# Down-projection of a fourier / RG-LRU / ConvFFN block: low parts and sums on VectorE alone, first steps prepared during the last up-products

## The chip, the core and the metric

[...] The metric is device time in microseconds of one execution.

## The reference

One layer of a diffusion block over 1024 latent positions of width 1024, in float32. The change lies in its second half, the ConvFFN:

```python
def conv_ffn(h, rows, w_up, conv_w, conv_b, w_down):
    b, n, _ = h.shape
    u = (h @ w_up).reshape(b, rows, n // rows, 2 * D_FF)          # D_FF = 2816
    u = dwconv2d(u, conv_w, conv_b).reshape(b, n, 2 * D_FF)       # 3x3 depthwise on a 16 x 64 grid
    gate, val = jnp.split(u, 2, axis=-1)
    return (jax.nn.gelu(gate) * val) @ w_down
...
x = x + g2 * conv_ffn(modulate(x, norm2_g[l], sh2, sc2), rows,
                      ffn_w_up[l], ffn_conv_w[l], ffn_conv_b[l], ffn_w_down[l])
return rms_norm(x, final_g)
```

## The kernel before

**Products in three matmuls.** A float32 operand is split into a high part (a copy to the matmul type fp32r, ScalarE, `copy`, line 131) and a low part (operand minus high part, `sub`, line 138, on VectorE or GpSimd). A product is high x high + high x low + low x high.

**Seven products instead of eight.** Up- and down-projection each use a Strassen-Winograd scheme: two-by-two blocks of both operands, sums of blocks, seven block products, sums of results.

**Up-projection** (`ffn`). The 2816 gate and 2816 value channels go in 22 tiles n of 128 channels. Tile n has two PSUM tiles, `ug` (gate) and `uv` (value), of 1024 positions, and seven products i = 0 to 6 of twelve matmuls (`up_product`, line 1526). Product 6 of tile n runs after product 0 of tile n+1. `up_join` (line 1542, VectorE) adds a stored product to half a PSUM tile; `up_conv` starts the 3x3 convolution: one ScalarE instruction for the centre and eight "taps" on VectorE that read PSUM and add to the accumulator in SBUF (line 1564). `gelu` (ScalarE), then `glu` (line 1574, GpSimd) multiplies gate and value, and the result goes to DRAM, G[n] (line 1576). At the last tile `up_free` gives back the operands of a finished product and starts the loads of the down weights.

**Down-projection** (`down`). The 22 channel tiles of G form 11 pairs i of an even and an odd tile. Seven passes p, in the order `DOWN = (1, 2, 6, 7, 5, 4, 3)`, run over the 11 pairs: 77 steps s, each a 128 x 512 by 128 x 512 product with four position blocks j, twelve matmuls (`mm`, line 1792). X and Y are sets of four PSUM banks (`dn`): passes 1, 2 and then 5, 3 collect in X, passes 6, 7, 4 in Y, which begins as a copy of X after pass 1. A step's operands go through four stages, each run ahead of the matmuls by `down_until`:

- `down_load`: the weight tile (line 1679), the activations (1688, 1693, 1696), the stored sum S2 (1697), on SP's queue, up to six steps ahead;
- `down_sums`: the sums of blocks, mostly VectorE (two operations in pass 2, three in pass 6, one in passes 7, 5 and 3); one of pass 6 on GpSimd (line 1714);
- `down_hi`: two high parts on ScalarE;
- `down_lo`: two low parts, the first on GpSimd, the second on VectorE, three steps ahead.

All these buffers are 48 slots that are handed out again in the order in which they were given back. Between the stages of a step stand at most two "tasks" from a list: evacuations of PSUM, multiplications by the row g2, additions to the residual rows y (fetched from DRAM by `fetch`, line 1770), squares (ScalarE, line 1779), and `norm` (lines 1782 to 1785), the final RMSNorm of 128 positions and its store. The last four steps of pass 3 are run block by block: all matmuls of j = 0, then of j = 1 and so on, and a last block of code finishes each j.

What sets the order: each engine's list is the order in which this code calls it. In pass 1 the last taps, step by step, stand between the stages, and the last up-product stands ahead of step 0.

Of the kernel before, what the change touches and what calls it, by code (L numbers as in the profile page):

```python
# [11 lines left out]
OP = mybir.AluOpType  # L12
# [100 lines left out]
class K:  # L113
# [1471 lines left out]
    def ffn(self):  # L1585
        sl = self.sl
        self.G = [self.dp.tile([128, 1024], F32, name=f"G{n}") for n in range(NP)]
        last = NP - 1

        todo = deque([(0, 4), (0, 5), (0, 6), (1, 1), (1, 3), (1, 4), (1, 5), (1, 6)])  # L1590
        self.down_plan()
        for n in range(NP):
            if n > 1:
                self.up_banks(n)
            if n + 2 < NP and n:
                self.up_load(n + 2)
# [102 lines left out]
    def down_sums(self, s, p, i):  # L1699
# [52 lines left out]
    def down(self):  # L1752
# [4 lines left out]
        y = {}  # L1757
# [43 lines left out]
        for p in self.DOWN:  # L1801
            if p in (1, 5):
                X = banks()
            if p == 6:
                X, bank = X, Y
            bank = Y if p in (6, 7, 4) else X
            for i in range(11):
                if p == 1:
                    if i == 0:
                        self.up_product(last, 6)  # L1810
                        self.up_free(6)
                        self.up_conv(last, "v")
                    if i == 2:
                        self.glu(last - 1)
                        self.taps(last, "gt", 1)
                    self.taps(last, "gt" if i < 5 else "vt", 2 if i < 9 else 8)
                    if i == 5:
# [4 lines left out]
                self.down_until(self.down_load, s + 6 if p != 1 or i > 2 else s + 4)  # L1822
# [6 lines left out]
                if p == 7 and i == 0 or p == 5 and i == 0:  # L1829
                    pass  # L1830
                if i:
                    for _ in range(2):
                        if tasks:
                            tasks.popleft()()
                if p == 3 and i == 7:
                    for f in (self.down_hi, self.down_lo):
                        self.down_until(f, len(self.steps))
                    for j in range(4):
                        for q in range(4):
                            mm(s + q, X, [j], False, q == 3)  # L1840
# [8 lines left out]
            if p == 1:  # L1849
                Y = banks()  # L1850
                for j in range(4):
                    self.copy("act", Y[j], X[j])
            elif p == 2:
                for j in range(4):
                    c11[j] = temp(j)
                    tasks.append(lambda j=j, b=X[j]: v.tensor_tensor(c11[j], b, self.g2row[:, H[0]], op=OP.mult))
            elif p == 6:
                u = pair()
                for j in range(4):
                    self.copy("act", at(u, j), Y[j])  # L1860
            elif p == 7:
                def begin():
                    nonlocal w
# [1 line left out]
                tasks += [lambda: None] * 4 + [begin]  # L1865
                for j in range(4):
                    tasks.append(lambda j=j, b=Y[j]: self.copy("act", at(w, j), b))
            elif p == 5:
                fg = sl.get([128, 1024], any_=True)
                src = a["final_g"]  # L1870
                nc.sync.dma_start(fg, bass.AP(tensor=src.tensor, offset=src.offset, ap=[[0, 128], [1, 1024]]))
                p5 = pair()
                for j in range(4):
                    tasks.append(lambda j=j, b=X[j]: self.copy("act", at(p5, j), b))
                for j in range(4):
                    def c22(j=j):
                        g.tensor_tensor(at(w, j), at(w, j), at(p5, j), op=OP.add)
                        g.tensor_tensor(at(w, j), at(w, j), self.g2row[:, H[1]], op=OP.mult)

                    def c12(j=j):  # L1880
# [3 lines left out]
                    tasks += [c22, c12]  # L1884
                for j in range(4):
                    def adds(j=j):
                        v.tensor_tensor(y[j][:, H[1]], y[j][:, H[1]], at(u, j), op=OP.add)
                        v.tensor_tensor(y[4 + j][:, H[1]], y[4 + j][:, H[1]], at(w, j), op=OP.add)
                        square(4 + j, 1, j)
                    tasks.append(adds)  # L1890
            elif p == 4:
                r = [temp(j) for j in range(4)]
                for j in range(4):
                    tasks.append(lambda j=j, b=Y[j]: v.tensor_tensor(r[j], b, self.g2row[:, H[0]], op=OP.mult))
                for j in range(4):
                    def add(j=j):
                        v.tensor_tensor(y[4 + j][:, H[0]], y[4 + j][:, H[0]], r[j], op=OP.add)
                        square(4 + j, 0, j)
                    tasks.append(add)
                for j in range(4):  # L1900
                    tasks.append(lambda j=j: norm(4 + j))
        for j in range(4):
            r = temp(j)
            v.tensor_tensor(r, X[j], self.g2row[:, H[1]], op=OP.mult)
            v.tensor_tensor(y[j][:, H[1]], y[j][:, H[1]], r, op=OP.add)
            square(j, 1, j)
            norm(j)

    def run(self):
        self.plan()  # L1910
# [84 lines left out]
```

## Time and profile before

| | us |
|---|---|
| median of three runs (1555.39 to 1558.95) | 1557.04 |
| profiled execution, its own time | 1557.34 |
| its span, first to last instruction | 1555.5 |
| busy: TensorE / VectorE / GpSimd / ScalarE | 1408.2 / 1215.6 / 755.1 / 669.3 |
| mean granted clock of TensorE, as a share of full speed | 0.966 |

The down-projection begins at about 1272 us of the span and ends with it. "Busy" of TensorE counts modelled ends of pipelined matmuls; how fast it is fed is better read from the time that a pass takes. The mean of a whole run hides stages with different limits, so the views that follow are cut to the down-projection, and within it to passes and to single waits.

### The profile page before, as it was taken

To read this page: it belongs to the slowest core of one execution; us is meant where nothing else is said; L and a number is where in the kernel's file an instruction comes from. 1 tells how busy PE (TensorE), PEld (TensorE's weight loads), DVE (VectorE), ACT (ScalarE), POOL (GpSimd) and SP (SyncE) were. 2 spreads that over 40 slices of the span, in tenths; PEclk is the share of its full clock that TensorE was granted. 3 is DMA by queue.
4 is the path that set the end of the run, shared out by engine and by line. 5 is a ranking of instruction groups with operands and counts; after the bars stand their busy time and mean duration, and the time that the engine had idled before them with its cause. 6 is when DMAs were issued, how large, how long until landed. Compare 5 with 4: busy or idle time off the path is not lost.

```text
span 1555.5 us, 17031 instructions
## 1 busy us (share of the span) xinstructions
PE 1408.2 (91%) x6333; PEld 1126.9 (72%) x6333; DVE 1215.6 (78%) x1265; ACT 669.3 (43%) x968; POOL 755.1 (49%) x504
## 2 busy tenths in 40 slices
PE   5999999998999689979967999999999988989983
PEld 4788888877887678868845777777777767768862
DVE  5768677855116986495687999999999989799795
ACT  6566777663110213342255444444444434445441
POOL 2211311122002452392088777788777726886760
PEclk9999999999999899989988999999999998999996
DMA  9211111101115444413321112222211166422622
GB/s 374 94 34 34 35 34 41 41 28 55 41 54 180 136 126 160 154 41 122 111 80 54 66 61 78 82 82 82 82 63 64 51 243 230 183 75 102 230 88 103
DMA packets 52787, 155.21 MB, mean 100 GB/s; under 512 B 5781, under 2 KB 10192, under 8 KB 52704
## 3 DMA queue, kind: packets, MB, share of 16 engines
q1 hardware_dynamic: 51264, 151.76, 27.4%
q10 hardware_dynamic: 1184, 2.11, 0.4%
q8 instruction: 50, 0.82, 0.2%
q0 software_dynamic: 256, 0.25, 0.1%
q14 instruction: 33, 0.27, 0.1%
HBM read 131.29 MB, written 22.81 MB: 99 GB/s over the span
## 4 chain that ended last, share of the span: by engine, by line
DVE 36%; PE 13%; issue 6%; ACT 2%; POOL 1%; DMA 1%; SPq 0%; DVEq 0%; ACTq 0%; POOLq 0%
DVE s L1564 23%; PE big L194 6%; PE dn L1792 6%; DVE s L138 2%; POOL s L138 1%; DVE ug L1542 1%; DVE s L1713 1%; DVE uv L1542 1%; DVE s L1710 1%; DVE s L1225 1%; PE uv L1526 1%; DVE s L1784 1%; DMA s<-G 1%; ACT s L131 1%; DVE s L1726 1%
## 5 line engine op out<-in xcount | busy, mean ns | idle before, releaser
L138 POOL TENSOR_TENSOR s<-s,s 128x512 fp32r<-128x512 f32 (+1 forms) x288 | 462.0, 1621 | 332.4 <-ACT s L131 259.9
L194 PE MATMUL big<-s,s 128*128 128x512 f32 (+2 forms) x2352 | 559.2, 396 | 10.3 <-DVE s L138 6.5
L194 PEld LDWEIGHTS big<-s,s 128*128 128x128 f32 (+2 forms) x2352 | 438.0, 189 | 115.7 <-DVE s L138 7.8
L131 ACT ACTIVATE s<-s 128x512 fp32r<-128x512 f32 (+2 forms) x406 | 263.0, 697 | 259.8 <-DVE mid L912 61.9
L1526 PE MATMUL ug<-s,s 128*128 128x512 f32 x1056 | 263.9, 398 | 24.3 <-ACT uv L131 13.4
L138 DVE TENSOR_TENSOR s<-s,s 128x512 fp32r<-128x512 f32 (+2 forms) x150 | 189.8, 1274 | 92.1 <-ACT s L131 64.7
L1526 PEld LDWEIGHTS ug<-s,s 128*128 128x128 f32 x1056 | 197.7, 189 | 79.1 <-ACT uv L131 22.0
L1792 PE MATMUL dn<-s,s 128*128 128x512 f32 x924 | 227.9, 408 | 29.9 <-DVE s L138 15.5
L1792 PEld LDWEIGHTS dn<-s,s 128*128 128x128 f32 x924 | 180.0, 196 | 77.7 <-DVE s L138 17.5
L1564 DVE SCALAR_TENSOR_TENSOR s<-ug,rest,s 128x945 f32<-128x945 f32 (+2 forms) x176 | 214.9, 1221 | 5.3
L1564 DVE SCALAR_TENSOR_TENSOR s<-uv,rest,s 128x945 f32<-128x945 f32 (+2 forms) x176 | 214.8, 1220 | 4.6
L1526 PE MATMUL uv<-s,s 128*128 128x512 f32 x792 | 199.9, 402 | 15.3 <-DVE uv L1542 14.0
L1526 PEld LDWEIGHTS uv<-s,s 128*128 128x128 f32 x792 | 149.5, 191 | 59.1 <-DVE uv L1542 23.4
L782 POOL TENSOR_TENSOR s<-s,s 128x1280 f32<-128x1280 f32 x8 | 25.2, 3152 | 190.9 <-ACT s L778 190.9
L899 POOL TENSOR_TENSOR s<-s,s 128x1024 f32<-128x1024 f32 x8 | 21.1, 2641 | 127.4 <-PE big L194 120.7
L1474 POOL TENSOR_TENSOR s<-s,s 128x512 f32<-128x512 f32 x22 | 28.6, 1301 | 63.6 <-DMA s<-in_ffn_w_up_b_dram 63.6
L131 ACT ACTIVATE p<-uv 128x512 f32<-128x512 f32 x22 | 13.2, 599 | 105.5 <-PE uv L1526 105.5
L885 DVE TENSOR_TENSOR s<-big,s 128x1024 f32<-128x1024 f32 x8 | 9.8, 1224 | 61.1 <-PE big L194 61.1
L745 DVE SCALAR_TENSOR_TENSOR s<-big,par,s 128x1023 f32<-128x1023 f32 (+1 forms) x24 | 30.8, 1282 | 34.2 <-ACT s L742 33.6
L1574 POOL TENSOR_TENSOR s<-s,s 128x1024 f32<-128x1024 f32 x22 | 53.4, 2427 | 5.5 <-DVE s L1564 5.5
L1552 ACT ACTIVATE s<-uv,rest 128x1024 f32<-128x1024 f32 x22 | 26.6, 1208 | 48.2 <-POOL s L138 33.6
L777 ACT ACTIVATE s<-big,rest 128x1024 f32<-128x1024 f32 x32 | 35.7, 1117 | 24.6 <-PE big L194 17.8
(231 smaller groups left out, 1537.8 us busy)
## 6 DMA issues: line engine op xcount, KB each, us to landing
s<-in_mod_w_dram SPq DMA_DIRECT2D x48, 512.0 KB, 4.7
s<-in_ffn_w_up_b_dram SPq DMA_DIRECT2D x44, 512.0 KB, 4.3
s<-in_w_in_b_dram SPq DMA_DIRECT2D x32, 512.0 KB, 4.3
s<-G SPq DMA_DIRECT2D x55, 256.0 KB, 3.2
G<-s SPq DMA_DIRECT2D x22, 512.0 KB, 2.6
s<-in_ffn_w_down_dram SPq DMA_DIRECT2D x22, 512.0 KB, 5.8
s<-in_x_dram SPq DMA_DIRECT2D x16, 512.0 KB, 5.4
s<-G SPq DMA_DIRECT2D x11, 512.0 KB, 5.7
```

Source lines behind the costliest of these rows:

```text
L131: self.nc.scalar.activation(out, in_, AF.Copy)
L138: (self.nc.vector if eng == "dve" else self.nc.gpsimd).tensor_tensor(out, a, b, op=OP.subtract)
L194: return [lambda x=x: nc.tensor.matmul(x[0], x[1], x[2], start=x[3], stop=x[4]) for x in calls]
L745: nc.vector.scalar_tensor_tensor(u[:, lo:hi], z[:, lo + s:hi + s], tap[t], u[:, lo:hi], op0=OP.mult, op1=OP.add)
L777: nc.scalar.activation(lat, ps, AF.Sigmoid, bias=col)
L1474: p.tensor_tensor(u["x"][:, L], rg[:, L], rv[:, L], op=OP.subtract)
L1526: nc.tensor.matmul(o, x, y, start=first, stop=k == 3 and m == 2, skip_group_check=not fresh)
L1542: self.nc.vector.tensor_tensor(o, o, p, op=OP.add)
L1552: nc.scalar.activation(acc, ps, AF.Identity, bias=self.par["fcb"][:, ti:ti + 1], scale=self.fcw(4, ti))
L1564: nc.vector.scalar_tensor_tensor(o, i, w, o, op0=OP.mult, op1=OP.add))
L1574: nc.gpsimd.tensor_tensor(u["ga"], u["ga"], u["va"], op=OP.mult)
L1792: nc.tensor.matmul(bank[j], x, z, start=first and m == 0, stop=end and m == 2, skip_group_check=not check)
```

## The change

- **Low parts** (`down_lo`): both on GpSimd in pass 1 for the first nine pairs, both on VectorE in all other steps. The sum of pass 6 that GpSimd made (line 1714) goes to VectorE.
- **Start**: `up_free` now loads weights and activations of the first nine steps in turn, and prepares high and low parts of the first two or three. The last up-product moves from ahead of step 0 to behind it; the join of the value half moves behind that product. The taps of the last tile stand alone on VectorE up to pair 8.
- **Tasks**: the first evacuation by multiplication (`c11`) moves from after pass 2 to after pass 6; the multiplication of `u` goes from GpSimd to VectorE, behind pass 7; in pass 4 the four ScalarE copies of X are left out and VectorE adds X from PSUM; the residual rows are fetched earlier, 0 to 3 in pass 5 and 4 to 7 at the beginning of pass 4.
- **Last block**: `norm` of block j stands behind multiplication, addition and square of block j + 1.

```diff
@@ ffn
-            self.up_join(n, "v")
+            if n < last:
+                self.up_join(n, "v")
@@ up_free
-        for _ in range(3):
-            if len(self.wd) < 11:
-                self.down_weight(len(self.wd), 0)
+        n = (2, 6, 4, 8, 8, 9, 9)[i]
+        self.down_until(self.down_load, n)
+        if i in (4, 5):
+            for f in (self.down_hi, self.down_lo):
+                self.down_until(f, i - 2)
@@ down_sums, pass 6
-            self.nc.gpsimd.tensor_tensor(o[:, L], o[:, L], t[0], op=OP.subtract)
+            v.tensor_tensor(o[:, L], o[:, L], t[0], op=OP.subtract)
@@ down_lo
-        for t, f, eng in zip(self.ready[s], self.factors(s, p, i), ("pool", "dve")):
+        for t, f, eng in zip(self.ready[s], self.factors(s, p, i), ["pool" if p == 1 and i < 9 else "dve"] * 2):
@@ down
-                    if i == 0:
+                    if i == 1:
                         self.up_product(last, 6)
                         self.up_free(6)
+                        self.up_join(last, "v")
                         self.up_conv(last, "v")
                     if i == 2:
                         self.glu(last - 1)
-                        self.taps(last, "gt", 1)
-                    self.taps(last, "gt" if i < 5 else "vt", 2 if i < 9 else 8)
+                    if i < 9:
+                        self.taps(last, "gt" if i < 4 else "vt", 2 if i < 8 else 8)
...
-                    if i == 10:
+                    if i == 9:
                         self.glu(last)
...
-                if p == 4 and i in (0, 2, 4, 6):
-                    fetch(4 + i // 2)
-                    fetch(i // 2)
+                if p == 5 and i in (5, 6, 7, 8):
+                    fetch(i - 5)
+                if p == 4 and i in (0, 1, 2, 3):
+                    fetch(4 + i)
...
             elif p == 7:
...
+                for j in range(4):
+                    tasks.append(lambda j=j: v.tensor_tensor(at(u, j), at(u, j), self.g2row[:, H[1]], op=OP.mult))
             elif p == 5:
...
-                p5 = pair()
                 for j in range(4):
-                    tasks.append(lambda j=j, b=X[j]: self.copy("act", at(p5, j), b))
+                    def c22(j=j, b=X[j]):
+                        v.tensor_tensor(at(w, j), b, at(w, j), op=OP.add)
+                        v.tensor_tensor(at(w, j), at(w, j), self.g2row[:, H[1]], op=OP.mult)
+                    tasks.append(c22)
                 for j in range(4):
-                    def c22(j=j):
-                        g.tensor_tensor(at(w, j), at(w, j), at(p5, j), op=OP.add)
-                        g.tensor_tensor(at(w, j), at(w, j), self.g2row[:, H[1]], op=OP.mult)
-
-                    def c12(j=j):
-                        g.tensor_tensor(at(u, j), at(u, j), self.g2row[:, H[1]], op=OP.mult)
+                    def c1(j=j):
                         v.tensor_tensor(y[j][:, H[0]], y[j][:, H[0]], c11[j], op=OP.add)
+                        v.tensor_tensor(y[j][:, H[1]], y[j][:, H[1]], at(u, j), op=OP.add)
                         square(j, 0, j)
...
-        for j in range(4):
-            r = temp(j)
...
-            norm(j)
+        for j in range(5):
+            if j < 4:
+                r = temp(j)
...
+            if j:
+                norm(j - 1)
```

Three places show the new order. TensorE, where the up-projection ends (`uv` is the value half of the last tile, `dn` a down bank, `s_` a buffer; s_8714 is the operand of the last up-product), lines with + are new there:

```order
 L1526 MATMUL uv<-s_5758,s_8811 128x512
 L1526 MATMUL uv<-s_5757,s_8811 128x512
+L1795 MATMUL dn<-s_8943,s_8942 128x512 x12
 L1526 MATMUL uv<-s_5691,s_8714 128x512
 L1526 MATMUL uv<-s_5692,s_8714 128x512
```

Step 0 now stands between the last two up-products.

VectorE at the same place, before (L1542 the join, L1564 taps, L138 low parts of steps 0 to 2):

```order
L1542 TENSOR_TENSOR uv<-uv,u_8951 128x512
L1564 SCALAR_TENSOR_TENSOR s_8934<-ug,rest,s_8934 128x15x63
L1564 SCALAR_TENSOR_TENSOR s_8934<-ug,rest,s_8934 128x960
L138 TENSOR_TENSOR s_8983<-s_8830,s_8983 128x512
L138 TENSOR_TENSOR s_8987<-s_8832,s_8987 128x512
L138 TENSOR_TENSOR s_8991<-s_8834,s_8991 128x512
```

and now, the end of the same taps (L1708 and L1709 are the sums of pass 2, L138 the low parts of steps 9 and 10):

```order
L1564 SCALAR_TENSOR_TENSOR s_9020<-uv,rest,s_9020 128x15x63
L1564 SCALAR_TENSOR_TENSOR s_9020<-uv,rest,s_9020 128x960
L1564 SCALAR_TENSOR_TENSOR s_9020<-uv,rest,s_9020 128x15x63
L1708 TENSOR_TENSOR s_8832<-s_8832 128x512
L1709 TENSOR_TENSOR s_8830<-s_8830 128x512
L138 TENSOR_TENSOR s_9139<-s_9088,s_9139 128x512
L138 TENSOR_TENSOR s_9140<-s_9086,s_9140 128x512
L1708 TENSOR_TENSOR s_8836<-s_8836 128x512
```

No low part stands among the taps any more; the first on VectorE is that of step 9, behind all of them.

VectorE where the sums of pass 6 are made, before (L1710 and L1713 sums, L138 the second low part of a step; GpSimd makes the first and the third sum):

```order
L1710 TENSOR_TENSOR s_9424<-s_9424,s_8976 128x512
L1713 TENSOR_TENSOR s_9448<-s_9157,s_8832 128x512
L138 TENSOR_TENSOR s_9431<-s_9379,s_9431 128x512
L1710 TENSOR_TENSOR s_9448<-s_9448,s_8978 128x512
L1713 TENSOR_TENSOR s_9472<-s_9182,s_8834 128x512
```

and now (L1713, L1716, L1717 sums, L138 both low parts):

```order
L1713 TENSOR_TENSOR s_9424<-s_9424,s_8836 128x512
L1716 TENSOR_TENSOR s_9448<-s_9159,s_8834 128x512
L1717 TENSOR_TENSOR s_9159<-s_9159,s_9448 128x512
L138 TENSOR_TENSOR s_9430<-s_9381,s_9430 128x512
L138 TENSOR_TENSOR s_9431<-s_9379,s_9431 128x512
```

Three operations a step became five; GpSimd's list has no row left behind the product of gate and value of the last tile.

## Rows read from the trace of the kernel before

**Rows 1.** Groups by form, 1282 to 1530 us: busy us, mean ns, idle before.

```profile
L1792 PE MATMUL dn<-s,s 128*128 128x512 f32 x896 | 221.3, 409 | 29.9 <-DVE s L138 15.5 <-POOL s L138 12.1 <-ACT s L131 2.3
...
L138 POOL TENSOR_TENSOR s<-s,s 128x512 fp32r<-128x512 f32 x77 | 133.5, 1752 | 74.6 <-ACT s L131 74.6
L138 DVE TENSOR_TENSOR s<-s,s 128x512 fp32r<-128x512 f32 x77 | 86.3, 1131 | 19.5 <-ACT s L131 13.4 <-issue 6.0
```

**Rows 2.** Busy by stretch: passes 1, 2, 6, 7 and 5, 4, last wait.

```profile
core 0: us, PE busy (x) PEld busy (x) DVE busy (x) ACT busy (x) POOL busy (x), PEclk, DMA share, GB/s
1281.00:1323.60 42.60, 37.38 (x138) 29.30 (x138) 40.91 (x38) 19.29 (x35) 27.19 (x16) 0.84 0.61 223
1323.60:1359.10 35.50, 31.70 (x129) 25.16 (x129) 27.32 (x33) 13.32 (x24) 30.98 (x14) 0.95 0.46 171
1359.10:1395.40 36.30, 31.45 (x131) 23.77 (x130) 36.30 (x31) 13.15 (x23) 31.90 (x20) 1.00 0.27 94
1395.40:1456.50 61.10, 61.10 (x266) 49.66 (x266) 53.96 (x45) 31.10 (x57) 39.83 (x25) 1.00 0.40 138
1456.50:1492.50 36.00, 32.53 (x135) 26.02 (x134) 35.06 (x24) 15.61 (x36) 32.74 (x20) 0.95 0.45 162
...
1513.40:1537.20 23.80, 12.83 (x41) 9.45 (x41) 14.70 (x38) 2.94 (x8) 1.45 (x2) 0.71 0.22 89
```

**Rows 3.** Timeline where up- and down-projection meet: start us, us, engine.

```profile
1268.70 2.95 PE L1526 MATMUL uv<-s,s 128*128 128x512 f32 x12
...
1270.35 3.68 DVE L1564 SCALAR_TENSOR_TENSOR s<-uv,rest,s 128x945 f32<-128x945 f32 x3
...
1274.70 4.50 PE L1526 MATMUL uv<-s,s 128*128 128x512 f32 x12 [3.04 <-DVE uv L1542]
```

**Rows 4.** Timeline in pass 2, GpSimd and VectorE.

```profile
1324.26 10.90 POOL L138 TENSOR_TENSOR s<-s,s 128x512 fp32r<-128x512 f32 x1 [5.82 <-ACT s L131]
...
1327.94 0.68 DVE L1706 TENSOR_TENSOR s<-s 128x512 f32<-128x512 f32 x1
1328.54 0.68 DVE L138 TENSOR_TENSOR s<-s,s 128x512 fp32r<-128x512 f32 x1
```

**Rows 5.** Timeline in pass 6, one round of GpSimd and VectorE.

```profile
1347.70 0.68 DVE L138 TENSOR_TENSOR s<-s,s 128x512 fp32r<-128x512 f32 x1
...
1347.86 1.67 POOL L1714 TENSOR_TENSOR s<-s,s 128x512 f32<-128x512 f32 x1 [0.63 <-DVE s L1713]
1348.30 1.77 DVE L1710 TENSOR_TENSOR s<-s,s 128x512 f32<-128x512 f32 x1
1349.48 1.75 POOL L138 TENSOR_TENSOR s<-s,s 128x512 fp32r<-128x512 f32 x1
```

**Rows 6.** Groups during the up-projection, 1140 to 1240 us.

```profile
L138 POOL TENSOR_TENSOR s<-s,s 128x512 fp32r<-128x512 f32 x34 | 43.9, 1302 | 22.3 <-ACT s L131 22.3
...
L1564 DVE SCALAR_TENSOR_TENSOR s<-uv,rest,s 128x945 f32<-128x945 f32 (+2 forms) x39 | 47.6, 1221 | 1.1
```

**Rows 7.** Timeline behind the last tap: last product of gate and value.

```profile
1312.36 2.72 POOL L1574 TENSOR_TENSOR s<-s,s 128x1024 f32<-128x1024 f32 x1 [5.51 <-DVE s L1564]
1312.80 2.84 DVE L1706 TENSOR_TENSOR s<-s 128x512 f32<-128x512 f32 x1
```

**Rows 8.** Busy in a stretch of dense loads; last two columns DMA.

```profile
1303.00:1306.00 3.00, 3.00 (x14) 2.44 (x13) 2.96 (x4) 1.55 (x4) 3.00 (x3) 1.00 1.02 399
```

**Rows 9.** Timeline of the end: norms, last low part, last blocks.

```profile
1512.01 0.20 DVE L1782 TENSOR_SCALAR ss<-sq 128x1 f32<-128x1 f32 x1
...
1517.93 0.68 DVE L1726 TENSOR_TENSOR s<-s 128x512 f32<-128x512 f32 x1
...
1525.80 11.18 PE L1792 MATMUL dn<-s,s 128*128 128x512 f32 x38 [4.88 <-DVE s L138]
1531.47 0.69 DVE L1904 TENSOR_TENSOR r<-dn,s 128x512 f32<-128x512 f32 x1 [5.73 <-PE dn L1792]
...
1533.74 0.21 DVE L1782 TENSOR_SCALAR ss<-sq 128x1 f32<-128x1 f32 x1 [0.85 <-ACT r L1779]
```

More of the change, by code (lines that the diff above doesn't have):

```diff
@@ L1803, in down @@
                 X = banks()
-            if p == 6:
-                X, bank = X, Y
             bank = Y if p in (6, 7, 4) else X
@@ L1814, in down @@
                         self.glu(last - 1)
-                        self.taps(last, "gt", 1)
-                    self.taps(last, "gt" if i < 5 else "vt", 2 if i < 9 else 8)
+                    if i < 9:
+                        self.taps(last, "gt" if i < 4 else "vt", 2 if i < 8 else 8)
                     if i == 5:
                         self.gelu(last)
-                    if i == 10:
+                    if i == 9:
                         self.glu(last)
                         self.warm(AF.Sqrt)
-                self.down_until(self.down_load, s + 6 if p != 1 or i > 2 else s + 4)
+                self.down_until(self.down_load, s + 6)
                 self.down_until(self.down_sums, s + 5)
@@ L1825, in down @@
                 self.down_until(self.down_lo, s + (3 if p != 3 else 4))
-                if p == 4 and i in (0, 2, 4, 6):
-                    fetch(4 + i // 2)
-                    fetch(i // 2)
[L1829 to L1834, printed above, removed]
+                if p == 5 and i in (5, 6, 7, 8):
+                    fetch(i - 5)
+                if p == 4 and i in (0, 1, 2, 3):
+                    fetch(4 + i)
+                for _ in range(2 if i else 0):
+                    if tasks:
+                        tasks.popleft()()
                 if p == 3 and i == 7:
@@ L1837, in down @@
                         self.down_until(f, len(self.steps))
+                    while tasks:
+                        tasks.popleft()()
                     for j in range(4):
@@ L1852, in down @@
                     self.copy("act", Y[j], X[j])
-            elif p == 2:
-                for j in range(4):
-                    c11[j] = temp(j)
-                    tasks.append(lambda j=j, b=X[j]: v.tensor_tensor(c11[j], b, self.g2row[:, H[0]], op=OP.mult))
             elif p == 6:
@@ L1860, in down @@
                     self.copy("act", at(u, j), Y[j])
+                for j in range(4):
+                    c11[j] = temp(j)
+                    tasks.append(lambda j=j, b=X[j]: v.tensor_tensor(c11[j], b, self.g2row[:, H[0]], op=OP.mult))
             elif p == 7:
@@ L1867, in down @@
                     tasks.append(lambda j=j, b=Y[j]: self.copy("act", at(w, j), b))
+                for j in range(4):
+                    tasks.append(lambda j=j: v.tensor_tensor(at(u, j), at(u, j), self.g2row[:, H[1]], op=OP.mult))
             elif p == 5:
@@ L1871, in down, with c2 @@
                 nc.sync.dma_start(fg, bass.AP(tensor=src.tensor, offset=src.offset, ap=[[0, 128], [1, 1024]]))
-                p5 = pair()
                 for j in range(4):
-                    tasks.append(lambda j=j, b=X[j]: self.copy("act", at(p5, j), b))
+                    def c22(j=j, b=X[j]):
+                        v.tensor_tensor(at(w, j), b, at(w, j), op=OP.add)
+                        v.tensor_tensor(at(w, j), at(w, j), self.g2row[:, H[1]], op=OP.mult)
+                    tasks.append(c22)
                 for j in range(4):
-                    def c22(j=j):
-                        g.tensor_tensor(at(w, j), at(w, j), at(p5, j), op=OP.add)
-                        g.tensor_tensor(at(w, j), at(w, j), self.g2row[:, H[1]], op=OP.mult)
-                    def c12(j=j):
-                        g.tensor_tensor(at(u, j), at(u, j), self.g2row[:, H[1]], op=OP.mult)
+                    def c1(j=j):
                         v.tensor_tensor(y[j][:, H[0]], y[j][:, H[0]], c11[j], op=OP.add)
+                        v.tensor_tensor(y[j][:, H[1]], y[j][:, H[1]], at(u, j), op=OP.add)
                         square(j, 0, j)
-                    tasks += [c22, c12]
+                    tasks.append(c1)
                 for j in range(4):
-                    def adds(j=j):
-                        v.tensor_tensor(y[j][:, H[1]], y[j][:, H[1]], at(u, j), op=OP.add)
+                    def c2(j=j):
                         v.tensor_tensor(y[4 + j][:, H[1]], y[4 + j][:, H[1]], at(w, j), op=OP.add)
                         square(4 + j, 1, j)
-                    tasks.append(adds)
+                    tasks.append(c2)
             elif p == 4:
@@ L1895, in down, with c21 @@
                 for j in range(4):
-                    def add(j=j):
+                    def c21(j=j):
                         v.tensor_tensor(y[4 + j][:, H[0]], y[4 + j][:, H[0]], r[j], op=OP.add)
                         square(4 + j, 0, j)
-                    tasks.append(add)
+                    tasks.append(c21)
                 for j in range(4):
                     tasks.append(lambda j=j: norm(4 + j))
-        for j in range(4):
-            r = temp(j)
-            v.tensor_tensor(r, X[j], self.g2row[:, H[1]], op=OP.mult)
-            v.tensor_tensor(y[j][:, H[1]], y[j][:, H[1]], r, op=OP.add)
-            square(j, 1, j)
-            norm(j)
+        for j in range(5):
+            if j < 4:
+                r = temp(j)
+                v.tensor_tensor(r, X[j], self.g2row[:, H[1]], op=OP.mult)
+                v.tensor_tensor(y[j][:, H[1]], y[j][:, H[1]], r, op=OP.add)
+                square(j, 1, j)
+            if j:
+                norm(j - 1)
     def run(self):
```

## The prediction

> **What bounds the kernel now.** I read four views in this order: the groups by line and form inside the down-projection, the busy times by pass, the timeline at the worst waits, and the same forms where they run undisturbed. A "step" is one pass p and one pair i, twelve matmuls; s counts steps from 0 to 76, eleven to a pass.
>
> The groups say who keeps TensorE waiting [rows 1]: of 29.9 us idle before down-projection matmuls, 15.5 ended with a low part from VectorE and 12.1 with one from GpSimd. One subtraction of one shape costs 1752 ns on GpSimd and 1131 ns on VectorE on average. By pass [rows 2], passes 7 and 5 take 61.10 us together with TensorE busy throughout: 61.1 / 22 = 2.78 us is what a fed step costs. Pass 1 takes 42.6 us, pass 2 35.5, pass 6 36.3, pass 4 36.0, against 11 x 2.78 = 30.6. [...]
>
> The boundary from up to down is a wait of its own [rows 3]: the product before the last ends at 1268.70 + 2.95 = 1271.65, the last one waits 3.04 us for the join on VectorE, which stands behind three taps, and then takes 4.50 us instead of 2.95.
>
> Why the low parts are dear: in pass 2 VectorE issues two-input subtractions every 0.60 us, and one GpSimd subtraction that began among them takes 10.90 us [rows 4]. In pass 6 it goes the other way: a VectorE subtraction beside a GpSimd one takes 1.77 us, beside none 0.68 [rows 5]. The two engines shut each other out, and TensorE needs both results for each step.
>
> **The change, part by part.** Start from fed steps, and ask where VectorE, now alone, is slower than 2.78 us.
>
> Boundary and pass 1: before, 1271.65 to 1323.6, that is 51.95 us. After, step 0 stands ahead of the last up-product, its operands come from GpSimd and ScalarE, which then idle, and that product waits for no join. Only the second half of step 0's bank waits for the last tap of tile 20, over at 1270.35 + 3.68 = 1274.03 [rows 3]; the first half needs 1.39 us from 1271.65, so 1.0 us is lost. Up to step 8 both low parts are GpSimd's. During the up-projection it makes one in 1.30 us beside taps on VectorE, and these take 1.22 [rows 6], so the two do not shut each other out there: 2.6 us a step, under 2.78, with a head start since about 1267, when ScalarE has copied the product that ends two before 1271.65. The taps (six of the gate, eight of the value, 1.24 apart, starting after the last up-product, 1271.65 + 1.0 + 2 x 2.78 = 1278.2, and the join, 0.7) end at about 1296, against 1312 before [rows 7]; VectorE then has two sums and step 9's low parts to make (2.4 us) until TensorE wants step 9 at about 1300. So 12 x 2.78 + 1.0 + 0.5 for copies = 34.9; **gain 17.0**. If GpSimd cost its contended 1.75 a piece instead [rows 1], pass 1 would run at 18 x 1.75 + 2.7 for the product of gate and value from 1267.4, some 4 us behind, and 2 more at the low clock; I take 1.30, since taps are the only VectorE work there.
>
> Between taps and pass 2 stands one trap: tile 21's product of gate and value is GpSimd's last work, and begins just after VectorE has begun its row of subtractions. In the trace of before the same pair meets at that place: the product takes 2.72, one subtraction waits 2.84. I take that, and it fits into the slack. The loads of steps from 14 on stand behind the write of this product on SP's queue; at about 1299 that leaves over 10 us until step 14. Pass 2 then asks 0.79 MB a step, 283 GB/s, where one stretch moved 399 [rows 8].
>
> Pass 2: two sums and two low parts, 4 x 0.60 = 2.4 us, under 2.78: 30.6, **gain 4.9**. During it the sums of pass 6 begin: three sums and two low parts, one of them dependent on its neighbour, 3.1 us. That is 0.33 over a step, 3.6 us in eleven, against a lead of about 9 x 0.38 = 3.4 collected just before; I leave 1.2 for pass 6: 31.8 instead of 36.3, **gain 4.5**. Its bounds are 0 (all hidden) and 4 (no lead). Passes 7 and 5 need 1.8 to 3.0 us a step and were fed before: nothing. In pass 4 VectorE has two low parts (1.2) plus two tasks a step; from step 56 to 59 that is 3.6 to 3.8, from 60 on 2.4; the four steps overrun by about 4 us in all, while the low parts then stand three steps (8.3 us) ahead. Dropping the four copies, twelve GpSimd operations and their contention leaves 30.6 + 0.5; **gain 4.9**. The residual rows are fetched six to eight steps earlier and hide behind fed steps.
>
> Pass 3 to the last low part: before, from 1492.5, where the window of pass 4 ends [rows 2], to 1525.8 [rows 9], 33.3 us. After, VectorE has everything up to step 70 done when pass 4 ends; then follow, in its order, two pairs of evacuations, two of adds, and four groups of one sum and two low parts (4 x 1.2 + 4 x 1.8, the first pair 1.2 before the end): 10.8; two row norms, 5.92 (1512.01 to 1517.93) [rows 9]; a group, 1.8; two norms, 5.92; two low parts, 1.2. Together 25.6; **gain 7.7**. TensorE has reached the point where it needs them after 20.9 and waits 4.7, as it does now for 4.88, so the matmuls behind start at the low clock as now, and cost the same. The norms are not moved; this wait is what is late next.
>
> Tail: each of the last four blocks waits 0.85 us for ScalarE's square [rows 9]; the norms now stand one block later, so the square runs under the next block's multiply and add: 4 x 0.85, **gain 3.4**.
>
> Sum: 17.0 + 4.9 + 4.5 + 4.9 + 7.7 + 3.4 = 42.4. The profiled execution took 1557.34 us (span 1555.5; median of three 1557.04): 1557.3 - 42.4 = **1515**. About 0.2%, 3 us, is what a measurement of this kernel tells from no change.
>
> **The rivals.** (a) *GpSimd shut out at the seam.* If tile 21's product meets the fate of rows 4 and not of rows 7, it waits until VectorE runs dry, which is at step 14's low parts (about 1309), because their load stands behind its write. Then 2.4 for the product, 4 for the load, 2.5 for high and low parts: step 14 at 1318.5 instead of 1314, and about 2 at the low clock: +7, 1522. For it: rows 4; against: rows 7, the same two instructions. [...]
>
> (b) *VectorE falls short in several passes.* If an operation costs its busy 0.68 and not 0.60, pass 6 needs 3.5 us a step: 0.7 x 11 = 8 us; with the 1.75 of GpSimd in pass 1 (6 us) together 1529. For it: TensorE now depends on one engine; against: the distances in rows 4.
>
> (c) *Slower: VectorE becomes the bound.* If it cannot hold 0.60 but pays the average of rows 1, 1.13 an operation, then over 2.78 stand 1.7 x 11 in pass 2, 2.9 x 11 in pass 6, 0.6 x 22 in passes 7 and 5 and about 10 in pass 3: 74 us, 1589. It decides from about 0.95 an operation, where the overruns (11 + 22 + 2 + 6) eat the gain. For it: that average. Against: it mixes 0.68 and 1.77, and the 1.77 lie beside GpSimd [rows 5]. [...]
>
> (d) *No change:* TensorE's waits turn out to be loads or slots instead. Against: the fed passes 7 and 5 use the same slots and queue.
>
> **How the numbers follow.** Forecast 0.68; (a) 0.12; (b) 0.11; (c) 0.07; (d) 0.02. The likeliest gives 1515, with 1508 to 1521 from its bounds: pass 6 (+4, -1), a step at 2.73 as in the best stretches (67 x 0.05 = 3), no low clock at the last wait (-2), seams (+2). Range 1508 to 1530, which takes in (a) and nearly all of (b). Faster 0.91, same 0.02, slower 0.07.
>
> **What would show it.** In the profile after: no GpSimd work past about 1299; step 0 ahead of the last up-product; pass 1 near 35 us at a granted clock near 1.00; VectorE's 128x512 subtractions at a mean near 0.68; passes 2, 6 and 4 near 31; a last wait of 4 to 5 us ended by VectorE after the norms; tail blocks some 4.2 us apart. Wrong if the subtractions stay above 0.95, if step 14 waits for its load, or if TensorE still waits over 10 us between passes 1 and 4.

## The result

| | median us | range, us | ratio to before, 95% interval |
|---|---|---|---|
| before | 1556.93 | 1555.39 to 1558.95 | |
| after | 1514.56 | 1512.18 to 1516.26 | 0.9727 [0.9714, 0.9740] |

Forecast 1515, measured 1514.56. The profiled execution of after took 1516.26 us (span 1514.5). Its up-projection ends later than that of before: the product before the last ends at 1271.24 + 2.96 = 1274.20 instead of 1271.65, though the last products ahead of it run alike in both. Over the kernels of this study that moment lies anywhere from 1270.1 to 1274.2, so stretches are compared from there on. From there to the end of the span before took 283.85 us and after takes 240.3: 43.55 less, where the sum said 42.4.

The groups of after, by line and form from 1265 to 1500 us (busy us, mean ns, idle before), answer [rows 1]:

```profile
L1795 PE MATMUL dn<-s,s 128*128 128x512 f32 x924 | 216.3, 395 | 5.1 <-DVE s L138 4.0 <-DVE s L1564 1.1
...
L138 DVE TENSOR_TENSOR s<-s,s 128x512 fp32r<-128x512 f32 x136 | 86.9, 681 | 3.4 <-ACT s L131 3.4
L138 POOL TENSOR_TENSOR s<-s,s 128x512 fp32r<-128x512 f32 x18 | 22.8, 1300 | 13.1 <-ACT s L131 13.1
```

VectorE makes 136 low parts in 86.9 us; before, 77 cost it 86.3. One takes 0.68 us instead of 1.13, one of GpSimd's 18 takes 1.30 instead of 1.75, and TensorE waits 5.1 us instead of 29.9.

The busy times by stretch answer [rows 2]: boundary and pass 1, pass 2, pass 6, passes 7 and 5, pass 4, pass 3 and its wait, tail (columns: PE, PEld, VectorE, ScalarE, GpSimd, granted clock, DMA share, GB/s).

```profile
1274.20:1309.40 35.20, 33.67 (x146) 26.58 (x144) 32.47 (x33) 18.23 (x31) 23.65 (x17) 1.00 0.62 234
1309.40:1340.00 30.60, 30.60 (x133) 24.79 (x133) 30.46 (x51) 14.62 (x26) 0.00 (x0) 1.00 0.63 228
1340.00:1370.90 30.90, 30.90 (x135) 24.83 (x134) 30.66 (x51) 13.96 (x23) 0.00 (x0) 1.00 0.35 119
1370.90:1432.00 61.10, 61.10 (x265) 49.57 (x266) 45.13 (x74) 32.56 (x58) 0.00 (x0) 1.00 0.47 167
1432.00:1462.50 30.50, 30.50 (x134) 24.91 (x133) 30.39 (x51) 16.45 (x36) 0.00 (x0) 1.00 0.44 151
1462.50:1492.50 30.00, 26.39 (x109) 21.25 (x108) 23.04 (x52) 9.46 (x22) 0.00 (x0) 0.94 0.29 113
1492.50:1514.50 22.00, 5.54 (x24) 4.13 (x23) 14.35 (x36) 3.74 (x12) 0.00 (x0) 0.69 0.24 96
```

TensorE is busy throughout passes 2, 6, 7, 5 and 4, at a granted clock of 1.00. The timeline of TensorE shows all that is left of its waits (start us, us, the last column the idle time before and what ended it):

```profile
1274.05 1.55 PE L1795 MATMUL dn<-s,s 128*128 128x512 f32 x6
1276.69 1.60 PE L1795 MATMUL dn<-s,s 128*128 128x512 f32 x6 [1.10 <-DVE s L1564]
1278.13 2.91 PE L1526 MATMUL uv<-s,s 128*128 128x512 f32 x12
1280.88 22.57 PE L1795 MATMUL dn<-s,s 128*128 128x512 f32 x97
1303.88 180.11 PE L1795 MATMUL dn<-s,s 128*128 128x512 f32 x777 [0.43 <-DVE s L138]
1487.61 10.44 PE L1795 MATMUL dn<-s,s 128*128 128x512 f32 x38 [3.61 <-DVE s L138]
```

The two halves of step 0 stand ahead of the last up-product with 1.10 us between them, and that product takes 2.91 us where it took 4.50 behind a wait of 3.04 [rows 3].

### The profile page after: what moved, and what is told of

It is laid out like the page before. It is cut to its first block, busy times and chain, and to the rows that moved or that the text cites. A ratio compares the mean times of both kernels' runs of the same rounds, so it can differ in the third digit from the quotient of the medians.

```text
span 1514.5 us, 16967 instructions
## 1 busy us (share of the span) xinstructions
PE 1397.1 (92%) x6333; PEld 1122.0 (74%) x6333; DVE 1178.0 (78%) x1347; ACT 668.7 (44%) x964; POOL 606.7 (40%) x422
## 4 chain that ended last, share of the span: by engine, by line
DVE 35%; PE 18%; issue 5%; ACT 1%; DMA 0%; DVEq 0%; ACTq 0%
DVE s L1564 24%; PE dn L1795 9%; PE big L194 6%; DVE s L138 2%; PE uv L1526 1%; PE ug L1526 1%; DVE ug L1542 1%; DVE uv L1542 1%; DVE s L1225 1%; DVE s L1787 1%; PE big L1212 0%; DVE s L1366 0%; DVE t L1367 0%; DVE s L338 0%; DVE s L1729 0%
## 5 line engine op out<-in xcount | busy, mean ns | idle before, releaser
L138 POOL TENSOR_TENSOR s<-s,s 128x512 fp32r<-128x512 f32 (+1 forms) x229 | 351.3, 1551 | 273.2 <-ACT s L131 178.9
L138 DVE TENSOR_TENSOR s<-s,s 128x512 fp32r<-128x512 f32 (+3 forms) x209 | 190.2, 940 | 74.3 <-ACT s L131 53.1
L1795 PE MATMUL dn<-s,s 128*128 128x512 f32 x924 | 216.3, 395 | 5.1 <-DVE s L138 4.0
L1564 DVE SCALAR_TENSOR_TENSOR s<-ug,rest,s 128x945 f32<-128x945 f32 (+2 forms) x176 | 214.9, 1221 | 5.4
L1564 DVE SCALAR_TENSOR_TENSOR s<-uv,rest,s 128x945 f32<-128x945 f32 (+2 forms) x176 | 214.7, 1220 | 4.7
L1795 PEld LDWEIGHTS dn<-s,s 128*128 128x128 f32 x924 | 174.2, 189 | 46.9 <-DVE s L138 4.9
L745 DVE SCALAR_TENSOR_TENSOR s<-big,par,s 128x1023 f32<-128x1023 f32 (+1 forms) x24 | 30.8, 1282 | 34.2 <-ACT s L742 33.6
L885 DVE TENSOR_TENSOR s<-big,s 128x1024 f32<-128x1024 f32 x8 | 9.8, 1223 | 61.1 <-PE big L194 61.1
```

The source lines that it names most:

```text
L138: (self.nc.vector if eng == "dve" else self.nc.gpsimd).tensor_tensor(out, a, b, op=OP.subtract)
L745: nc.vector.scalar_tensor_tensor(u[:, lo:hi], z[:, lo + s:hi + s], tap[t], u[:, lo:hi], op0=OP.mult, op1=OP.add)
L1564: nc.vector.scalar_tensor_tensor(o, i, w, o, op0=OP.mult, op1=OP.add))
L1795: nc.tensor.matmul(bank[j], x, z, start=first and m == 0, stop=end and m == 2, skip_group_check=not check)
```

## Experiments

The kernel before ran beside each set of kernels, at medians of 1557.2 to 1559.0, so kernels are compared by their ratios to it. The column "by ratio" is the difference of ratio from after's 0.9727, times 1557; "by trace" is the stretch from the product named above to the end of the span, less after's 240.3.

| label | median us | ratio, 95% interval | by ratio, us | by trace, us |
|---|---|---|---|---|
| e1_lows_back | 1530.48 | 0.9814 [0.9798, 0.9831] | +13.5 | +18.8 |
| e2_lows_alone | 1538.85 | 0.9871 [0.9856, 0.9886] | +22.4 | +23.9 |
| e4_third_sum | 1519.16 | 0.9749 [0.9733, 0.9765] | +3.4 | +4.7 |
| e5_two_on_pool | 1526.43 | 0.9791 [0.9776, 0.9806] | +10.0 | +10.3 |
| e12_pause | 1515.50 | 0.9725 [0.9710, 0.9739] | -0.3 | +1.2 |
| e13_all_vector | 1527.91 | 0.9802 [0.9782, 0.9822] | +11.7 | +13.5 |
| e11_no_prep | 1520.23 | 0.9756 [0.9743, 0.9770] | +4.5 | +5.3 |
| e10_product_first | 1514.82 | 0.9722 [0.9708, 0.9735] | -0.8 | -0.4 |
| e6_tail_old | 1515.90 | 0.9739 [0.9726, 0.9752] | +1.9 | +2.1 |
| e7_sqrt_first | 1512.05 | 0.9711 [0.9699, 0.9724] | -2.5 | -1.6 |
| e8_norms_late | 1509.02 | 0.9693 [0.9680, 0.9706] | -5.3 | -5.0 |
| e9_both | 1508.34 | 0.9685 [0.9671, 0.9698] | -6.5 | -6.6 |

### Is it GpSimd's share of the low parts?

The theory: the two engines shut each other out, and the later passes waited for that. The rival: the earlier start and the new order brought the gain. e1 undoes the one part in after, e2 does it alone in before, e4 undoes a piece of it.

e1_lows_back:

```diff
-            v.tensor_tensor(o[:, L], o[:, L], t[0], op=OP.subtract)
+            self.nc.gpsimd.tensor_tensor(o[:, L], o[:, L], t[0], op=OP.subtract)
...
-        ... ["pool" if p == 1 and i < 9 else "dve"] * 2):
+        ... ["pool", "pool" if p == 1 and i < 9 else "dve"]):
```

> The changed kernel, with the first low part of each step outside pass 1 and the third sum of pass 6 given back to GpSimd; the new start, the late copies and the shifted norms stay. Theory one (the two engines shut each other out, and the passes after the first waited for that): the waits of passes 2, 6, 4 and 3 come back, of the 22.0 us predicted for them (4.9 + 4.5 + 4.9 + 7.7) some 15 to 20, so 1530 to 1535, with VectorE's 128x512 subtraction at a mean near 1.0 us again. Rival (the gain is the start and the new order of the work, and GpSimd with a lead would do as well): at most 1518.

Measured 1530.48, as the theory said (the profiled execution, the +18.8 of the table, is the slowest of four: they lie between 1529.6 and 1533.87). Groups of e1 by line and form, 1265 to 1515 us:

```profile
L1795 PE MATMUL dn<-s,s 128*128 128x512 f32 x922 | 221.6, 401 | 18.1 <-POOL s L138 9.2 <-DVE s L138 7.7 <-DVE s L1564 1.1
...
L138 POOL TENSOR_TENSOR s<-s,s 128x512 fp32r<-128x512 f32 x86 | 149.1, 1759 | 59.7 <-ACT s L131 59.7
...
L138 DVE TENSOR_TENSOR s<-s,s 128x512 fp32r<-128x512 f32 x68 | 73.4, 1085 | 7.1 <-POOL s L138 6.6 <-ACT s L131 0.6
```

VectorE has half as many low parts as in after and still needs 73.4 us for them: 1.09 each. The prices of [rows 1] are back, and 18.1 us of waits with them, 5.1 in after. The theory expected them in passes 2, 6, 4 and 3. From its first matmul to the first of the next pass, pass 2 takes 38.2 us (after 30.7) and pass 6 36.2 (30.6), but pass 4 takes 30.35 as in after (before 35.81). It lies in this piece of TensorE's timeline, without a wait:

```profile
1376.30 120.59 PE L1795 MATMUL dn<-s,s 128*128 128x512 f32 x521 [0.92 <-POOL s L138]
```

e2_lows_alone, the kernel before with:

```diff
-            self.nc.gpsimd.tensor_tensor(o[:, L], o[:, L], t[0], op=OP.subtract)
+            v.tensor_tensor(o[:, L], o[:, L], t[0], op=OP.subtract)
...
-        for t, f, eng in zip(self.ready[s], self.factors(s, p, i), ("pool", "dve")):
+        for t, f, eng in zip(self.ready[s], self.factors(s, p, i), ["pool" if p == 1 else "dve", "dve"]):
```

> The kernel before, with only the low parts outside pass 1 and the third sum of pass 6 moved to VectorE; start, copies and norms as before. Theory one (mutual exclusion in the passes): passes 2, 6 and 4 fall from about 36 to 31 or 32 us each and pass 3 by some 3, so 1539 to 1543. Rival (the gain is the start and the new order): 1552 or more, since one engine has more to do and nothing starts earlier.

Measured 1538.85, just under the theory's range, ratio 0.9871: 20.1 us off the kernel before, 19.6 by the traces. The rival's 1552 is out. TensorE's timeline, from pass 1 to the waits of pass 3:

```profile
1316.54 179.36 PE L1792 MATMUL dn<-s,s 128*128 128x512 f32 x762 [2.86 <-DVE s L138]
```

So moving the low parts brings 20 us when it is done alone, and 13.5 (by ratio) to 18.8 us (by trace) on top of the rest, out of 42.4: nearly half at most. The other parts are worth 283.85 - 259.1 = 24.7 us against before (e1's stretch; 29 by ratio), a good half of it at the boundary and in pass 1. Pass 4 shows that the two don't simply add. It is fed in e1, without the copies and GpSimd's other operations there, and in e2 (30.52 us), without GpSimd's low parts: either the low parts or the rest of the change would have gained its 5 us alone.

e4_third_sum, after with the first half of e1's edit (line 1717) only.

> The changed kernel, with only the third sum of pass 6 (eleven subtractions) on GpSimd. Theory one: one VectorE operation a step is held up by 1.1 us (1.77 against 0.68) for 0.6 us of work taken off, and GpSimd's own result comes late behind VectorE's row, so the low part that needs it does too: 1516 to 1521. Rival (unloading VectorE counts for more): 1513 to 1515.

Measured 1519.16. Eleven subtractions off VectorE make the kernel slower. The ratio's interval touches that of after, so the size rests on the trace: pass 6 takes 34.8 us instead of 30.6. In the groups of e4 the low parts of VectorE take 0.74 on average instead of 0.68, and the eleven on GpSimd 2.60. That mean hides two cases: the first of the eleven takes 11.86 us, the other ten 1.5 to 1.75.

```profile
L138 DVE TENSOR_TENSOR s<-s,s 128x512 fp32r<-128x512 f32 x136 | 94.7, 737 | 4.2 <-ACT s L131 4.2
...
L1717 POOL TENSOR_TENSOR s<-s,s 128x512 f32<-128x512 f32 x11 | 28.4, 2600 | 35.5 <-DVE s L1716 27.2 <-ACT s L131 7.6 <-DMA S<-s 0.8
```

### How is GpSimd shut out?

e5 puts two low parts into pass 2's row of VectorE subtractions; e12 adds to that a few one-operand instructions between them.

e5_two_on_pool:

```diff
-        ... ["pool" if p == 1 and i < 9 else "dve"] * 2):
+        ... ["pool" if p == 1 and i < 9 or s in (14, 17) else "dve", "pool" if p == 1 and i < 9 else "dve"]):
```

> The changed kernel, with only the first low part of steps 14 and 17 on GpSimd, both in the stretch of pass 2 where VectorE subtracts without a pause. Theory A (a GpSimd instruction is held out as long as VectorE's row goes on, as in rows 4): each of the two takes over 5 us in the records, TensorE waits for it unless VectorE comes to a halt first; 1516 to 1526. Theory B (it is held out for one instruction of VectorE at most): each takes 2.5 us at most, TensorE waits for neither, 1514 to 1515.

e12_pause, besides:

```diff
         if p == 2:
+            if i >= 6:
+                v.tensor_scalar(self.pause, self.pause, 1.0, 0.0, op0=OP.mult, op1=OP.add)
             v.tensor_tensor(g[:, L], g[:, L], g[:, R], op=OP.subtract)
```

> The kernel with two low parts of pass 2 on GpSimd again, and besides five one-operand instructions of VectorE on 128x1 elements, 0.15 us each, between its subtractions, ahead of the sums of the pairs 6 to 10. Theory one (GpSimd comes in as soon as VectorE runs something that is not a two-operand subtraction): the first GpSimd low part, 15.9 us without them, ends some 5.5 us after it began, TensorE waits for neither, 1514 to 1516.5. Theory two (only a VectorE that stands still lets it in): it again lasts until VectorE halts, 13 to 16 us, and the time stays at 1524 to 1527.

e5 took 1526.43, e12 1515.50. First e5: its two GpSimd low parts as one tile's instructions (count, shortest/median/longest ns, first and last start), then the timeline of GpSimd, VectorE, TensorE and ScalarE.

```profile
L138 POOL TENSOR_TENSOR s<-s,s x2: 1287/8612/15937, 1310.1 to 1326.0; 128x512 fp32r<-128x512 f32 x2
```

```profile
1310.11 17.19 POOL L138 TENSOR_TENSOR s<-s,s 128x512 fp32r<-128x512 f32 x2 [9.21 <-ACT s L131]
...
1324.25 0.67 DVE L138 TENSOR_TENSOR s<-s,s 128x512 fp32r<-128x512 f32 x1
1330.73 0.69 DVE L138 TENSOR_TENSOR s<-s,s 128x512 fp32r<-128x512 f32 x1 [5.81 <-ACT s L131]
...
1326.10 6.20 PE L1795 MATMUL dn<-s,s 128*128 128x512 f32 x20 [8.82 <-POOL s L138]
...
1330.07 1.15 ACT L131 ACTIVATE s<-s 128x512 fp32r<-128x512 f32 x2 [10.91 <-PE dn L1795]
```

The first takes 15.94 us: it begins at 1310.11 and ends 1.1 us after VectorE's last subtraction (1324.25 + 0.67 = 1324.92). And VectorE comes to a halt only because its next low part waits for a ScalarE copy, and this for TensorE, which waits 8.82 us for GpSimd. The row of subtractions ends only once TensorE stands still. The second low part then takes 1.29, so that the expectation of over 5 us for each held for the first alone.

The same place in e12:

```profile
1307.21 6.81 POOL L138 TENSOR_TENSOR s<-s,s 128x512 fp32r<-128x512 f32 x2 [9.25 <-ACT s L131]
...
1311.07 0.14 DVE L1710 TENSOR_SCALAR pause<-pause 128x1 f32<-128x1 f32 x1
1311.14 1.72 DVE L1711 TENSOR_TENSOR s<-s 128x512 f32<-128x512 f32 x1
1312.78 1.79 DVE L1712 TENSOR_TENSOR s<-s 128x512 f32<-128x512 f32 x1
1314.49 1.28 DVE L138 TENSOR_TENSOR s<-s,s 128x512 fp32r<-128x512 f32 x2
```

One instruction of 0.14 us that reads one small operand ends the shut-out: the two-operand subtraction behind it takes 1.72 us instead of 0.68, GpSimd's first low part ends after 5.1, and TensorE waits for neither. VectorE didn't have to stand still here; one instruction other than the next two-operand subtraction was enough. It isn't free: VectorE lets GpSimd in twice, and comes to the sums of pass 6 1.3 us later than in after (1324.97 - 1270.07 = 54.90 us behind the product named above, instead of 1327.84 - 1274.20 = 53.64). The 1.72 and 1.79 us here each stand beside one GpSimd low part; the 15.94 us of e5 lasted through 24 of VectorE's subtractions, and the 10.90 of [rows 4] through 16.

### What is the start worth?

e13_all_vector gives GpSimd's low parts of pass 1 to VectorE too; e11_no_prep drops the preparation during the last up-products; e10_product_first puts the last up-product ahead of step 0 again.

```diff
-        ... ["pool" if p == 1 and i < 9 else "dve"] * 2):
+        ... ("dve", "dve")):
```

> The changed kernel, with GpSimd's 18 low parts of pass 1 on VectorE as well. They add 18 x 0.60 = 10.8 us to VectorE in pass 1, so the taps of the last tile end at about 1307 instead of 1296.6, and what hangs on them (the product of gate and value, its write, the load of step 14) comes 10 us later. Theory one (GpSimd's help in pass 1 carries part of the gain): TensorE waits in pass 1 or at step 14, 1517 to 1523. Rival (VectorE, with some 57 us of work in the 61 us of passes 1 and 2, has room): 1513.5 to 1515.5.

Measured 1527.91, worse than either theory. TensorE's timeline in e13:

```profile
1278.93 1.61 PE L1795 MATMUL dn<-s,s 128*128 128x512 f32 x6 [3.54 <-DVE s L1564]
1280.37 4.51 PE L1526 MATMUL uv<-s,s 128*128 128x512 f32 x12
...
1314.17 181.71 PE L1795 MATMUL dn<-s,s 128*128 128x512 f32 x777 [3.90 <-DVE s L138]
```

The rival's count of VectorE's work may be right, but the order of it leaves no room. The low parts of the first steps stand ahead of the taps, so the tap that step 0 needs comes 2.4 us later (3.54 instead of 1.10), and step 9 waits 3.90 us where it waited 0.43. GpSimd's 18 low parts, at 1.30 each beside taps, are worth about 12 us. "VectorE alone" is right from pass 2 on, not in pass 1, as the order of the code stands.

```diff
-        if i in (4, 5):
-            for f in (self.down_hi, self.down_lo):
-                self.down_until(f, i - 2)
```

> The changed kernel, without the preparation of the first steps' high and low parts during the last up-products. The first step then waits for a copy on ScalarE and a subtraction on GpSimd (about 0.8 + 1.3 us at the boundary, then a low clock), and the head start of GpSimd is gone: 1517 to 1520. Rival (the preparation is hidden anyway behind the last product): 1514 to 1515.

Measured 1520.23. In e11 step 0 waits first for ScalarE, then for GpSimd:

```profile
1274.61 0.49 PE L1792 MATMUL dn<-s,s 128*128 128x512 f32 x1 [1.72 <-ACT s L131]
1276.68 4.33 PE L1792 MATMUL dn<-s,s 128*128 128x512 f32 x11 [1.58 <-POOL s L138]
```

That is 3.30 us of waits, and eleven matmuls in 4.33 us, where twelve of a fed step take 2.78.

```diff
-                    if i == 1:
+                    if i == 0:
```

> The changed kernel, with the last up-product ahead of step 0 again, its operands, the join's place and all else as in the changed kernel. The prediction put 1.0 us of idle time between the halves of step 0; with the product first there is no such wait, but step 0 comes one product later and the taps begin earlier: 1513.5 to 1515.5. If the order is what spares TensorE the wait for the join: 1516 to 1518.

Measured 1514.82, no difference from after. With the product first TensorE waits 0.69 us for a copy instead of 1.10 for a tap. So the order of step 0 and the product brings nothing. That the operands are ready counts, as e11 shows; that the product no longer waits for the join holds in both orders, and what this and the earlier loads bring by themselves no run shows.

### The end

e6_tail_old puts the norm of each of the last blocks back into its block, e7_sqrt_first calls it ahead of the next square, e8_norms_late puts the four norms of blocks 4 to 7 behind the last low parts, e9_both is e7 and e8 together.

```diff
@@ e7_sqrt_first @@
-                square(j, 1, j)
             if j:
                 norm(j - 1)
+            if j < 4:
+                square(j, 1, j)
@@ e8_norms_late @@
-                    while tasks:
-                        tasks.popleft()()
+                    for j in range(4):
+                        norm(4 + j)
...
-                for j in range(4):
-                    tasks.append(lambda j=j: norm(4 + j))
```

> The changed kernel, with the norm of each of the last four blocks back in its own block. The prediction gave this part 4 x 0.85 = 3.4 us; the trace of the changed kernel, where each block now waits 0.91 us for the square root that stands behind the next square on ScalarE, says about 2: 1516.5 to 1518.

> The changed kernel, with the norm of the block before called ahead of the square of the next one, so that its square root is ahead of that square on ScalarE. If the 0.91 us waits for the square root are what the tail has lost, they go and the square hides under the norm: 1512.5 to 1513.5. Rival (the square then comes late and the wait moves to the next norm): 1514 to 1516.

> The changed kernel, with the four row norms of blocks 4 to 7 behind the last low parts instead of between them. Theory (two norms of 5.54 us each time stand ahead of the last low parts, and TensorE waits 3.6 us for them): no wait, no low clock behind it, and the norms run while TensorE finishes, 1509.5 to 1511. Rival (the norms then delay the evacuations of the last blocks on VectorE): 1513 to 1517.

> The changed kernel, with both of the last two edits: norms behind the last low parts, and the square root ahead of the next square. If both gains stand they add: 1508 to 1510. If the delayed norms hold up the tail: 1512 to 1515.

Measured 1515.90, 1512.05, 1509.02 and 1508.34, the first three up to 0.6 us below what was expected. The intervals of e6 and e7 overlap that of after, so their sizes rest on the traces: 2.1 us longer and 1.6 shorter. VectorE's timeline in one block of after's tail, then of e7's:

```profile
1499.83 0.21 DVE L1785 TENSOR_SCALAR ss<-sq 128x1 f32<-128x1 f32 x1
1500.94 0.15 DVE L453 TENSOR_SCALAR ss<-ss 128x1 f32<-128x1 f32 x1 [0.91 <-ACT t L450]
...
1504.48 0.20 DVE L1785 TENSOR_SCALAR ss<-sq 128x1 f32<-128x1 f32 x1
```

```profile
1498.26 0.21 DVE L1785 TENSOR_SCALAR ss<-sq 128x1 f32<-128x1 f32 x1
1498.83 0.15 DVE L453 TENSOR_SCALAR ss<-ss 128x1 f32<-128x1 f32 x1 [0.36 <-ACT t L450]
...
1502.37 0.21 DVE L1785 TENSOR_SCALAR ss<-sq 128x1 f32<-128x1 f32 x1
```

A block takes 4.65 us in after and 4.11 in e7; before it took 5.04 (from one norm's first instruction to the next, 1533.74 [rows 9] to 1538.79). In after the square no longer holds VectorE up, but the square root of the norm stands behind the next square on ScalarE.

In e8 TensorE runs from step 9 to its last matmul in one piece:

```profile
1303.76 188.95 PE L1795 MATMUL dn<-s,s 128*128 128x512 f32 x815 [0.43 <-DVE s L138]
```

The wait of 3.61 us is gone, and so is the low granted clock behind it. The 4.9 us before the first evacuation of the last blocks, in after and then in e8 (columns as above, the clock behind the five engines):

```profile
1487.60:1492.50 4.90, 4.89 (x15) 3.97 (x16) 0.00 (x0) 0.00 (x0) 0.00 (x0) 0.69 0.19 75
```

```profile
1482.40:1487.30 4.90, 4.90 (x23) 3.98 (x22) 4.25 (x13) 0.30 (x1) 0.00 (x0) 1.00 0.54 219
```

In the same time TensorE does 15 matmuls at a mean granted clock of 0.69 and 23 at 1.00. The low clock that the forecast reckons with behind a wait is 0.50 in the trace of before (3 us windows from 1282 to 1288 us, behind the waits at the boundary). e9 joins both edits at ratio 0.9685, faster than before and than after.

## Why the prediction was right, and where it was not

| term | before | after | gain | forecast |
|---|---|---|---|---|
| boundary, pass 1 | 51.95 | 35.2 | 16.75 | 17.0 |
| passes 2 and 6 | 71.8 | 61.5 | 10.3 | 9.4 |
| passes 7 and 5 | 61.1 | 61.1 | 0 | 0 |
| pass 4 | 36.0 | 30.5 | 5.5 | 4.9 |
| pass 3 to the last wait | 33.3 | 25.1 | 8.2 | 7.7 |
| behind the last wait | 29.7 | 26.9 | 2.8 | 3.4 |
| sum | 283.85 | 240.3 | 43.55 | 42.4 |

**The mechanism** held. The choice of 0.60 us between subtractions, from [rows 4], was the main one, and VectorE alone keeps it through pass 2. Rival (c) falls with that, and (d) with the waits that are gone. e1 and e2 show from both sides that the two engines' shutting each other out cost 13.5 to 20 us of the 42.4; a good half of the rest is the start, of which e13 and e11 show parts. That the total came within half a microsecond is partly luck: the terms miss by -0.6 to +0.9 us, together they fall 1.15 short, and the later end of the up-projection in after's profiled execution (2.55 us) goes the other way.

**Boundary and pass 1**: the 1.0 us between the halves of step 0 was 1.10, GpSimd's low parts cost 1.30, and pass 1 ran at a granted clock of 1.00. The taps end at about 1299.1, that is 24.9 after the product, where the forecast had 24.4 (1296 after 1271.65). e13 and e11 show that GpSimd's low parts and the prepared operands both carry it.

**Pass 6** was one mis-sized term: I left 1.2 us as a reserve, and the lower bound, 0, is what came. The working behind it came out. VectorE is slower than TensorE there, 3.13 us a step for a fed 2.78, and lives on the lead from pass 2. The low parts of steps 19 and 30 on VectorE, and the matmuls that TensorE has begun by 1331.70 and 1362.30, that is 19 and 30 steps of twelve:

```profile
1326.63 1.28 DVE L138 TENSOR_TENSOR s<-s,s 128x512 fp32r<-128x512 f32 x2
1361.10 1.28 DVE L138 TENSOR_TENSOR s<-s,s 128x512 fp32r<-128x512 f32 x2
1274.05:1331.70 57.65, 53.53 (x228) 1.00 0.65 241
1274.05:1362.30 88.25, 84.14 (x360) 1.00 0.59 214
```

The lead of the low parts over TensorE is 0.32 us at step 10. At step 19, behind which VectorE begins groups with three sums, it is 3.86 (1327.91 against 1331.77): 3.5 collected, where the sum said 3.4. It is used up at step 30, whose low parts end at 1362.38 while TensorE begins it at 1362.35, with a matmul of high parts alone: 3.9 spent, where the sum said 3.6. So the overrun was hidden by a margin of tenths, and that it was hidden wholly is luck. e12 shows what is behind it: there VectorE comes 1.3 us later to these sums, and TensorE's piece from step 9 to the last wait is 1.23 us longer than after's 180.11:

```profile
1299.77 181.34 PE L1798 MATMUL dn<-s,s 128*128 128x512 f32 x777 [0.43 <-DVE s L138]
```

**Pass 3**: two norms take 5.54 us, not 5.92, which is 0.8 of the 1.1 us by which TensorE waits less than the 4.7 of the sum (3.61). e8 shows that the norms ahead of the last low parts are the cause, and the price: about 5 us with the low clock behind it.

**Tail**: the step that failed is "4 x 0.85". The square is hidden as I said, but I did not follow ScalarE's queue to its next instruction: the square root of the norm now waits behind that square, 0.91 us instead of 0.36 each time. The part is worth 2.1 us by e6's trace. The rest of the 2.8 gained behind the last wait is the first evacuation, which comes 4.91 us after TensorE goes on (1487.61 to 1492.52), where it came 5.67 after [rows 9].

**Rival (a)** did not occur. Where the last tap ends, after shows the pattern of [rows 7]:

```profile
1299.29 2.78 POOL L1574 TENSOR_TENSOR s<-s,s 128x1024 f32<-128x1024 f32 x1 [2.97 <-DVE s L1564]
...
1299.13 0.68 DVE L1708 TENSOR_TENSOR s<-s 128x512 f32<-128x512 f32 x1
1299.73 2.90 DVE L1709 TENSOR_TENSOR s<-s 128x512 f32<-128x512 f32 x1
```

GpSimd comes in behind the first subtraction. e5 shows that the danger was real twelve microseconds later. Rival (b) did not occur either: 0.60 and 1.30 held.

## What to carry to other kernels

Between two engines that shut each other out, moving work to the idle one can cost more than it takes off (here eleven subtractions moved in e4 cost 4.7 us by trace): read the mean duration of one form alone and beside the other engine (here 0.68 and 1.77 us for VectorE's subtraction, [rows 5]) before sharing it out. Where both must be used, put GpSimd's work beside VectorE instructions that don't shut it out (here taps, which read one operand from PSUM; a GpSimd low part takes 1.30 us beside them), or break the row with another instruction (here one of 0.14 us on one small operand, in e12). When a wait is moved behind later work, follow every engine's queue one instruction further than the wait itself.

## What the runs showed of the hardware

A GpSimd subtraction that arrives while VectorE runs two-operand subtractions without a pause can be served not next but last: 10.90 us [rows 4], 15.94 in e5, 12.06 in e1, 11.86 in e4. Each ends 1.1 to 1.2 us after VectorE's last subtraction of the row (in the trace of before that one ends at 1333.36 + 0.68 = 1334.04, GpSimd's at 1335.16). One 0.14 us instruction on one operand let it in (e12), where it ended 5.1 us after its start. Once it had come in, the two took turns at 1.67 to 1.77 us each in [rows 5].

What stays open is when a newcomer is let in at once. The product at the seam gets in behind one subtraction, 0.16 us after the start of the first behind a tap. So do GpSimd's sums in pass 6 [rows 5], 0.16 us after the start of a subtraction in a row that goes on, after 0.63 us of idling. The moment alone does not decide: in e4 the sum that takes 11.86 us comes 0.21 us after the start of a subtraction, and so do later ones that take 1.62. In pass 6 of before and of e4 the two had taken turns shortly before; whether that is the reason, no run shows.
